# One trunk layer on one core: input tiles as 128 contiguous rows, reordered by the transposes; a bias table without its second copy in HBM; identity transposes at the start

## The chip, the cores and the metric

The kernel runs on one NeuronCore of a Trainium2 chip. A core has TensorE (PE), VectorE (DVE), ScalarE (ACT), GpSimd (POOL), a synchronisation engine (SP) that issues most DMAs, and 16 DMA engines. The time is that of the device, in microseconds (us), from launch to end. The kernel before was timed three times: 862.17, 866.29 and 864.95 us, median 864.95.

## The reference

One layer of a transformer on 128 prompt tokens and 512 sample tokens of width 1024, all in float32:

```
for each group (prompt: c_ctx; sample: c):
    sh1, sc1, gt1, sh2, sc2, gt2 = split(silu(cond) @ w_mod + b_mod, 6)       # w_mod 1024 x 6144
    h = rmsnorm(x, g_mix_pre) * (1 + sc1) + sh1
    qa, ka, va, qb, kb, vb = split(h @ w_in)                                 # w_in 1024 x 2304
    oa = 8 heads: prompt full attention; sample 2-D neighbourhood attention + cached keys
    ob = 8 heads: prompt full attention with a sink; sample window attention + rope + cached keys
    x = x + gt1 * rmsnorm(concat(rmsnorm(oa), rmsnorm(ob)) @ w_out)
    u = conv3(rmsnorm(x, g_ffn_pre) * (1 + sc2) + sh2) @ w_up ...            # w_up 1024 x 5632
    x = x + gt2 * rmsnorm((silu(gate) * val) @ w_down)                       # w_down 2816 x 1024
```

The sample tokens form a grid of 8 rows by 64 columns (token = row * 64 + column). Neighbourhood attention adds a bias to each score that depends on the row and column distance of query and key: `rpb_a[head, drow, dcol]`, 8 heads of 15 by 31 numbers; keys whose column is out of reach get a large negative number.

## The kernel before

The layer runs in stages, one after the other on the same core: loads, normalisation and transposition of x; the modulation and the V projection ("V phase"); q, k and attention of the neighbourhood heads, then of the window heads; the output projection; the FFN's first and second half. Products are made of three float32r products each, with every operand split into a high and a low part (`split`: ACT writes the high part, DVE or POOL the low).

**Token order.** Inside the kernel the sample tokens are in the order (j, r, c): 8 column blocks j of 8 columns, in each 8 rows r of 8 columns c. So 128 tokens in that order are two column blocks with all eight rows. `xnT[kb]` holds the normalised x transposed: 128 features on the partitions, 640 tokens along the row.

**The start (L174 to L326).** `load_xt(t)` brings tile t of x, 128 tokens by 1024 features, to `xs`. For the sample it makes two DMAs of 64 rows: `xsj[2 * t + jj]` picks the 8 x 8 tokens of one column block, and its outermost dimension has 8 entries. `x_norm(t)` squares and sums a tile on ACT, makes 1/rms on POOL and scales the tile on DVE. `x_trans(t)` transposes eight blocks of 128 x 128 on PE into two PSUM tiles `pxs`, which ACT and DVE copy to `xnT`. Small parameter rows (`load_rows`) come by DMAs of their own.

**The V phase (L458 to L500).** For each of eight blocks k of 128 features, PE makes two modulation products from `wm[k]` (two tiles of 512 KB; `ada_a`, `psada`), turns them to columns (`ada_c`, `pscol`), DVE makes G and S from them, ACT and DVE make h of block k (`hidden`), and 15 products go into the five V tiles `pv_` (`psv`). The V weights `vw[0..3]` are split by `vw_split`. The modulation of block k + 2 is made in the course of block k. `stream` brings the q/k weights (`wst`).

**The bias table.** `load_scr` (called at k = 4) scales `rpb_a` by 8 into `rpx`, rows of 48 numbers, in two versions v (0: columns out of reach are negative, 1: all 31 columns), and writes each version 16 times to `scr` in HBM. `load_ftab` copies `scr` to `ftab` in HBM by 1920 runs of 32 numbers for each v, with a start that moves by one number for each of the 16 copies. `load_traw(h)` reads four times 64 runs of 256 numbers from `ftab` for head h, with a start that depends on the query's column, to `traw`. `tab_ops(h)` puts `traw` in the order of the scores (`tab`), by copies on ACT and DVE for heads 0 and 1, on POOL for the others.

**What sets the order.** From the start to the end of the first q/k projection, the instructions of each engine run in the order in which the code is written (`manual_schedule`). SP issues its DMAs in that order too; a DMA waits in SP's queue until its buffer is free and until an older DMA that uses the same one of eight completion slots has landed. Behind it a scheduler orders the attention; the FFN is written out by hand again. Weight tiles have two buffers `ws0` and `ws1`, taken in turn, so `wst` of index 1 waits for the split of `vw[3]`.

## Time and profile before

| | |
|---|---|
| median of three runs | 864.95 us |
| the profiled execution's own time | 862.87 us |
| its span (first to last instruction) | 861.1 us |
| PE busy | 805.4 us (94%) |
| DVE, ACT, POOL busy | 563.5, 435.3, 305.5 us |
| moved by DMA | 107.77 MB, 125 GB/s over the span |
| mean granted TensorE clock | 0.983 |

One execution was profiled. Times in the views count from the span's start. A row of the timeline shows start, duration, engine, line and operation, then what is written and read, and in brackets how long the engine had been idle before and what ended that; a group of several equal instructions has one row, with their count. "SPq" and "ACTq" are the times in which SP or ACT issue a DMA, not the transfer. In the rows by stretch, the DMA share is the mean busy share of the 16 DMA engines. Matmul rows overlap, since PE is pipelined.

### The profile page before, as it was taken

How to read it: one execution, taken by the hardware profiler on the slowest of the kernel's cores; microseconds unless marked ns; L12 is line 12 of the kernel's file. 1: busy time of each engine (PE TensorE's matmuls, PEld its weight loads, DVE VectorE, ACT ScalarE, POOL GpSimd, SP SyncE). 2: the span in 40 equal slices, each digit the busy share in tenths (PEclk: the TensorE clock that was granted, in tenths of full speed). 3: DMA queues.
4: the chain of work that ended last, by engine and by line, in shares of the span. 5: the costliest groups of instructions: out<-in, count | busy, mean ns of one | idle time of the engine just before them, and what ended most of it. 6: DMA issues, size and time to landing. Idle time of an engine off the chain costs nothing.

```text
span 861.1 us, 13868 instructions
## 1 busy us (share of the span) xinstructions
PE 805.4 (94%) x5280; PEld 706.3 (82%) x5280; DVE 563.5 (65%) x1023; ACT 435.3 (51%) x876; POOL 305.5 (35%) x353
## 2 busy tenths in 40 slices
PE   2897999999999999999998999999999999999996
PEld 2666878888778777868898999999999987888885
DVE  1543466655788885476588898898998874422115
ACT  3443467746568786466535455455455544322112
POOL 2443144424121211155965565665665300000002
PEclk9999899999999998999999999999999999999999
DMA  6996644363522022656323332432432326434313
GB/s 152 264 234 117 169 144 126 109 175 97 134 74 74 26 74 61 213 173 188 105 65 93 116 114 83 126 113 80 128 113 83 119 101 228 170 112 159 120 49 122
DMA packets 144277, 107.77 MB, mean 125 GB/s; under 512 B 16440, under 2 KB 125268, under 8 KB 144212
## 3 DMA queue, kind: packets, MB, share of 16 engines
q1 hardware_dynamic: 143204, 106.25, 41.9%
q8 instruction: 41, 0.67, 0.3%
q10 hardware_dynamic: 1008, 0.66, 0.3%
q14 instruction: 24, 0.20, 0.1%
HBM read 93.02 MB, written 14.36 MB: 125 GB/s over the span
## 4 chain that ended last, share of the span: by engine, by line
PE 43%; DVE 30%; DMA 10%; ACT 8%; issue 5%; POOL 4%; SPq 1%; DVEq 0%; ACTq 0%; POOLq 0%
PE psd L127 16%; PE psg L127 9%; DVE cv L120 7%; DVE ou L111 5%; DVE cv L111 4%; DVE owl L111 3%; PE psya L127 3%; POOL fg L111 3%; PE psS L127 2%; PE zx L127 2%; ACT cv L108 2%; PE psyb L127 2%; DVE yy L111 2%; DMA wms<-in_w_mod_dram 2%; DMA scr<-rpx 2%
## 5 line engine op out<-in xcount | busy, mean ns | idle before, releaser
L127 PE MATMUL psd<-dwh,a 128*128 128x512 f32 x440 | 138.3, 395 | 0.0
L111 POOL TENSOR_TENSOR wsum<-wraw 128x512 f32<-128x512 f32 x36 | 78.7, 2204 | 93.7 <-DVE oc L111 86.1
L127 PE MATMUL zx<-h2H,ou 128*128 128x322 f32 x392 | 96.0, 314 | 7.2 <-DVE cv L120 4.0
L127 PEld LDWEIGHTS psd<-dwh,a 128*128 128x128 f32 x440 | 82.9, 188 | 19.8
L127 PE MATMUL psd<-dwl,a 128*128 128x512 f32 x220 | 87.2, 396 | 0.0
L127 PE MATMUL psg<-hH,wh 128*128 128x320 f32 x224 | 76.6, 342 | 8.4 <-ACT T L108 3.6
L111 DVE TENSOR_TENSOR dwl<-wd,dwh 128x1024 fp32r<-128x1024 f32 x22 | 26.9, 1224 | 86.6 <-ACT dwh L108 86.6
L127 PEld LDWEIGHTS zx<-h2H,ou 128*128 128x128 f32 x392 | 68.4, 190 | 9.6 <-DVE yy L111 5.4
L127 PE MATMUL psg<-hH,wl 128*128 128x320 f32 x224 | 71.0, 317 | 0.0
L127 PE MATMUL psg<-hL,wh 128*128 128x320 f32 x224 | 71.0, 317 | 0.0
L108 ACT ACTIVATE dwh<-wd 128x1024 fp32r<-128x1024 f32 x22 | 23.3, 1059 | 91.2 <-PE psd L127 85.5
L117 POOL TENSOR_SCALAR rdv<-ssdc 128x1 f32<-128x1 f32 x5 | 1.6, 328 | 177.3 <-ACT jk L108 177.3
L127 PE MATMUL zx<-h2L,ou 128*128 128x322 f32 x196 | 61.1, 312 | 0.0
L127 PEld LDWEIGHTS psg<-hH,wh 128*128 128x128 f32 x224 | 43.5, 194 | 17.5 <-issue 7.2
L108 ACT ACTIVATE cv<-yy,T 128x642 f32<-128x642 f32 x20 | 17.7, 886 | 67.2 <-DVE yy L111 67.2
L127 PEld LDWEIGHTS psd<-dwl,a 128*128 128x128 f32 x220 | 41.3, 188 | 10.3 <-DVE dwl L111 0.5
L120 DVE SCALAR_TENSOR_TENSOR cv<-yy,T,cv 128x641 f32<-128x641 f32 x40 | 35.4, 884 | 17.9 <-ACT cv L108 17.2
L111 POOL TENSOR_TENSOR wl<-wst,wh 128x1024 fp32r<-128x1024 f32 (+1 forms) x12 | 27.7, 2311 | 50.5 <-ACT wh L108 34.0
L127 PEld LDWEIGHTS psg<-hL,wh 128*128 128x128 f32 x224 | 43.6, 195 | 0.5
L127 PEld LDWEIGHTS psg<-hH,wl 128*128 128x128 f32 x224 | 43.4, 194 | 0.0
L111 DVE TENSOR_TENSOR ou<-wraw,ou 128x1024 fp32r<-128x1024 f32 x19 | 41.4, 2177 | 1.5 <-ACT ou L108 1.5
L108 ACT ACTIVATE P<-P,nm 128x320 f32<-128x320 f32 (+3 forms) x64 | 40.3, 630 | 3.9 <-DVE nm L639 3.8
(352 smaller groups left out, 2217.6 us busy)
## 6 DMA issues: line engine op xcount, KB each, us to landing
wraw<-in_w_up_dram SPq DMA_DIRECT2D x40, 512.0 KB
wms<-in_w_mod_dram SPq DMA_DIRECT2D x32, 512.0 KB
wd<-in_w_down_dram SPq DMA_DIRECT2D x22, 512.0 KB
wm<-in_w_mod_dram SPq DMA_DIRECT2D x16, 512.0 KB
aD<-cv SPq DMA_DIRECT2D x22, 321.0 KB
ar<-aD SPq DMA_DIRECT2D x11, 642.0 KB
wst<-in_w_in_dram SPq DMA_DIRECT2D x10, 512.0 KB
yD<-Y SPq DMA_DIRECT2D x5, 512.0 KB
```

What stands on the lines that cost most here:

```text
L108: return nc.scalar.activation(out=out, in_=in_, func=func, **kw)
L111: return (eng or nc.vector).tensor_tensor(out=out, in0=a, in1=b, op=op)
L117: return e.tensor_scalar(out=out, in0=a, scalar1=s1, scalar2=s2, op0=op0, op1=op1)
L120: return nc.vector.scalar_tensor_tensor(out=out, in0=a, scalar=s, in1=b, op0=op0, op1=op1)
L127: return nc.tensor.matmul(out, l, r, start=start, stop=stop, skip_group_check=True, **kw)
```

## The change

- x tiles: one DMA of 128 contiguous rows (two grid rows of 64 tokens) for each of the four sample tiles. The order (j, r, c) is made afterwards: a transpose of such a tile writes PSUM in runs of 8 columns (j, r, c with two rows r), and the copies to `xnT` put 16 tokens into each of the eight column blocks.
- The first loads stand in another order in SP's queue, and the first two parameter rows are transposed one tile earlier.
- 24 transposes of the identity stand first in PE's queue.
- The bias rows are stored backwards in 32 numbers a row (`rpx`), in one copy (`scr`, 2 x 8 x 512 numbers); `ftab` is gone, `load_traw` reads its runs from `scr`, and the table copies read them with a step of -1. `load_scr` is called at k = 1; `load_traw(0)` and `(1)` at k = 4.

```diff
 def load_xt(t):
-    if t == 4:
-        nc.sync.dma_start(out=xt[4], in_=xp)
-    else:
-        for jj in range(2):
-            nc.sync.dma_start(out=xt[t][jj * 64:jj * 64 + 64, :], in_=xsj[2 * t + jj])
-
-PW = 48
-rpx_ = PT([8, 2, 15, PW], "rpx")
-rpx = [rpx_[:, v] for v in range(2)]
-for v in range(2):
-    nc.gpsimd.memset(rpx[v], NEG)
+    nc.sync.dma_start(out=xt[t], in_=(xp if t == 4 else xs[t * 128:t * 128 + 128, :]))
+
+rpx = PT([8, 2, 512], "rpx")
+nc.gpsimd.memset(rpx, NEG)
...
-scr = dr_.tile([2, 16, 120, PW], F32, name="scr")
-ftab = dr_.tile([2, 16, 120 * 32], F32, name="ftab")
+scr = dr_.tile([2, 8, 512], F32, name="scr")
...
 def load_scr():
-    ts(rpx[0][:, :, 15:31], rev(rp, 7, 16), 8.0, None, ALU.mult)
-    ts(rpx[1][:, :, 8:39], rev(rp, 0, 31), 8.0, None, ALU.mult)
-    for v in range(2):
-        nc.sync.dma_start(
-            out=scr[v].rearrange("q (h a) w -> h q (a w)", h=8),
-            in_=rpx[v].rearrange("p a w -> p (a w)").unsqueeze(1).to_broadcast([8, 16, 720]),
-        )
-
-def load_ftab():
-    for v in range(2):
-        sv = scr[v, 0]
-        nc.sync.dma_start(
-            out=ftab[v].rearrange("q (a k) -> q a k", k=32),
-            in_=bass.AP(tensor=sv.tensor, offset=sv.offset + 15, ap=[[120 * PW - 1, 16], [PW, 120], [1, 32]]),
-        )
+    rv = [rpx[:, v, 0:480].rearrange("p (a w) -> p a w", w=32) for v in range(2)]
+    ts(rv[0][:, :, 16:32], rev(rp, 22, 16), 8.0, None, ALU.mult)
+    ts(rv[1][:, :, 0:31], rev(rp, 30, 31), 8.0, None, ALU.mult)
+    nc.sync.dma_start(out=scr.rearrange("v h w -> h v w"), in_=rpx)
...
-                in_=bass.AP(tensor=fv.tensor, offset=fv.offset + jj * 8 * 3840 + h * 480,
-                            ap=[[32, 8], [3840, 8], [1, 256]]))
+                in_=bass.AP(tensor=sv.tensor, offset=sv.offset + jj * 8, ap=[[32, 8], [1, 8], [1, 256]]))
...
-            nc.tensor.transpose(ps[:, i * 128:i * 128 + 128], xt[t][:, k * 128:k * 128 + 128], ident)
-        dst = xnT[kb][:, :, t * 128:t * 128 + 128]
-        src = ps.rearrange("p (k t) -> p k t", k=4)
+            o_ = ps[:, i * 128:i * 128 + 128]
+            if t < 4:
+                o_ = o_.rearrange("p (j r c) -> p r j c", j=8, r=2)
+            nc.tensor.transpose(o_, xt[t][:, k * 128:k * 128 + 128], ident)
+        if t == 4:
+            dst, src = xnT[kb][:, :, 512:640], ps.rearrange("p (k t) -> p k t", k=4)
+        else:
+            dst = xnT[kb][:, :, 0:512].rearrange("p k (j w) -> p k j w", j=8)[:, :, :, 16 * t:16 * t + 16]
+            src = ps.rearrange("p (k j w) -> p k j w", k=4, j=8)
...
+ps = PS("o", "warm")
+for i in range(24):
+    nc.tensor.transpose(ps[:, i % 4 * 128:i % 4 * 128 + 128], ident, ident)
 x_norm(0)
...
+    if k == 1:
+        load_scr()
...
     if k == 4:
-        load_scr()
-        load_ftab()
         stream.load()
         load_cc(0)
-    if k == 5:
         load_traw(0)
         load_traw(1)
...
-            src = bass.AP(tensor=b_.tensor, offset=b_.offset + 7 * 32 + j0 * 8,
-                          ap=[list(b_.ap[0]), [8, nj], [-32, 8], [1, 8]])
+            src = bass.AP(tensor=b_.tensor, offset=b_.offset + 7 * 32 + (23 if v else 31) - j0 * 8,
+                          ap=[list(b_.ap[0]), [-8, nj], [-32, 8], [-1, 8]])
```

How the queues stand before and after is shown at three places. First, SP's queue at the start of the kernel before (each row is a DMA: line, what is written from what, its shape; `xs_128` to `xs_130` are pairs of x tiles, `rows_127` the parameter rows, `wm_...` the modulation weights):

```order
L205 DMA xs_128<-in_x_sample_dram 64x1x1024 x4
L205 DMA xs_129<-in_x_sample_dram 64x1x1024 x2
L198 DMA rows_127<-in_c_ctx_dram 8x128
L198 DMA rows_127<-in_c_dram 8x128
L205 DMA xs_129<-in_x_sample_dram 64x1x1024 x2
L234 DMA wm_146<-in_w_mod_dram 128x8x128 x2
L202 DMA xs_130<-in_x_prompt_dram 128x1024
L198 DMA rows_127<-in_b_mod_dram 48x128
L198 DMA rows_127<-in_g_mix_pre_dram 8x128
L198 DMA sel<-in_sel_c_dram 128x2
L238 DMA vw<-in_w_in_dram 128x2x512
L234 DMA wm_155<-in_w_mod_dram 128x8x128 x2
```

and after the change:

```order
L200 DMA xs_128<-in_x_sample_dram 128x1024
L197 DMA rows_127<-in_c_ctx_dram 8x128
L197 DMA rows_127<-in_c_dram 8x128
L200 DMA xs_128<-in_x_sample_dram 128x1024
L200 DMA xs_129<-in_x_sample_dram 128x1024 x2
L200 DMA xs_130<-in_x_prompt_dram 128x1024
L197 DMA rows_127<-in_b_mod_dram 48x128
L197 DMA rows_127<-in_g_mix_pre_dram 8x128
L197 DMA sel<-in_sel_c_dram 128x2
L226 DMA wm_144<-in_w_mod_dram 128x8x128 x2
L230 DMA vw<-in_w_in_dram 128x2x512
L226 DMA wm_149<-in_w_mod_dram 128x8x128 x2
```

All five x tiles now stand ahead of the first modulation tile, and the first `vw` still between the first two. Behind these rows the second `vw` and the loads of `rp` and `sink` have moved ahead of the third and fourth modulation tiles.

Second, SP's queue around the bias table, before:

```order
L238 DMA vw<-in_w_in_dram 128x2x512
L350 DMA wst<-in_w_in_dram 128x8x128
L246 DMA scr<-rpx 8x16x720 x2
L254 DMA ftab<-scr 1920x1x32 x2
L350 DMA wst<-in_w_in_dram 128x8x128
L454 DMA cc<-in_cache_a_k_dram 128x128
L455 DMA cc<-in_cache_a_v_dram 128x128
L266 DMA traw_710<-ftab 64x1x256 x4
L266 DMA traw_715<-ftab 64x1x256 x4
```

and after:

```order
L238 DMA scr<-rpx 8x2x512
L230 DMA vw<-in_w_in_dram 128x2x512
L338 DMA wst<-in_w_in_dram 128x8x128 x2
L442 DMA cc<-in_cache_a_k_dram 128x128
L443 DMA cc<-in_cache_a_v_dram 128x128
L247 DMA traw_675<-scr 64x1x256 x4
L247 DMA traw_680<-scr 64x1x256 x4
L247 DMA traw_984<-scr 64x1x256 x4
L821 DMA wms<-in_w_mod_dram 128x8x128
```

The second `wst` now directly follows the first, with no bias table between them, and `traw` of the third head (`traw_984`) stands ahead of the next weights.

Third, PE's queue at the start, before:

```order
L306 MATMUL pxs<-ident,xs_128 128x128 x8
L321 MATMUL psr_220<-ident,rows_127 128x16
L306 MATMUL pxs<-ident,xs_128 128x128 x8
L306 MATMUL pxs<-ident,xs_129 128x128 x8
L383 MATMUL psada<-wm_146,cpad 32x128 x16
L306 MATMUL pxs<-ident,xs_129 128x128 x8
L329 MATMUL psr_297<-ident,rows_127 128x72
L415 MATMUL pscol<-sel,m_sb 128x2 x2
L306 MATMUL pxs<-ident,xs_130 128x128 x8
L383 MATMUL psada<-wm_155,cpad 32x128 x16
```

and after:

```order
L303 MATMUL warm<-ident 128x128 x24
L309 MATMUL psr_219<-ident,rows_127 128x16
L290 MATMUL pxs<-ident,xs_128 128x2x8x8 x16
L290 MATMUL pxs<-ident,xs_129 128x2x8x8 x8
L371 MATMUL psada<-wm_144,cpad 32x128 x16
L290 MATMUL pxs<-ident,xs_129 128x2x8x8 x8
L317 MATMUL psr_316<-ident,rows_127 128x72
L403 MATMUL pscol<-sel,m_sb 128x2 x2
L290 MATMUL pxs<-ident,xs_130 128x128 x8
L371 MATMUL psada<-wm_149,cpad 32x128 x16
```

The first modulation products still stand between the transposes of tiles 2 and 3; the transposes' shapes are new, and the rest of PE's queue is as before to the kernel's end. ACT, DVE and POOL keep their orders too, but for the parameter rows, the scaling of `rpx`, and some table copies of the third head that POOL now makes ahead of memsets.

More of the change, by code (lines that the diff above doesn't have):

```diff
@@ L177, in trunk_kernel @@
     xt = [xp_[t // 2][:, t % 2, :] for t in range(5)]
-    xsj = xs.rearrange("(r j c) d -> j r c d", r=8, j=8, c=8)
     rows = [
@@ L200, in load_xt @@
     def load_xt(t):
-        if t == 4:
-            nc.sync.dma_start(out=xt[4], in_=xp)
-        else:
-            for jj in range(2):
-                nc.sync.dma_start(out=xt[t][jj * 64:jj * 64 + 64, :], in_=xsj[2 * t + jj])
-    PW = 48
-    rpx_ = PT([8, 2, 15, PW], "rpx")
-    rpx = [rpx_[:, v] for v in range(2)]
-    for v in range(2):
-        nc.gpsimd.memset(rpx[v], NEG)
+        nc.sync.dma_start(out=xt[t], in_=(xp if t == 4 else xs[t * 128:t * 128 + 128, :]))
+    rpx = PT([8, 2, 512], "rpx")
+    nc.gpsimd.memset(rpx, NEG)
     def rev(ap, o, n):
-        return bass.AP(tensor=ap.tensor, offset=ap.offset + 14 * 31 + o, ap=[list(ap.ap[0]), [-31, 15], [1, n]])
-    scr = dr_.tile([2, 16, 120, PW], F32, name="scr")
-    ftab = dr_.tile([2, 16, 120 * 32], F32, name="ftab")
+        return bass.AP(tensor=ap.tensor, offset=ap.offset + 14 * 31 + o, ap=[list(ap.ap[0]), [-31, 15], [-1, n]])
+    scr = dr_.tile([2, 8, 512], F32, name="scr")
     wm = {}
@@ L264, in load_traw @@
             for jj in range(2):
-                fv = ftab[v]
+                sv = scr[v, h]
                 nc.sync.dma_start(
                     out=t[jj * 64:jj * 64 + 64, v, :],
-                    in_=bass.AP(tensor=fv.tensor, offset=fv.offset + jj * 8 * 3840 + h * 480,
-                                ap=[[32, 8], [3840, 8], [1, 256]]))
+                    in_=bass.AP(tensor=sv.tensor, offset=sv.offset + jj * 8, ap=[[32, 8], [1, 8], [1, 256]]))
     load_xt(0)
+    load_rows(2)
     load_xt(1)
     load_xt(2)
-    load_rows(2)
     load_xt(3)
-    load_wm(0)
     load_xt(4)
     load_rows(3)
+    load_wm(0)
     load_vw(0)
     load_wm(1)
+    load_late()
+    load_vw(1)
     load_wm(2)
-    load_vw(1)
     load_wm(3)
-    load_late()
     load_rows(6)
@@ L312, in x_trans @@
                 act(dst, src)
+    ps = PS("o", "warm")
+    for i in range(24):
+        nc.tensor.transpose(ps[:, i % 4 * 128:i % 4 * 128 + 128], ident, ident)
     x_norm(0)
-    for t in range(1, 5):
-        if t == 4:
-            break
+    for t in range(1, 4):
         x_norm(t)
-        if t == 2:
+        if t == 1:
             ps = PS("o", "psr1")
```

## The prediction, made before the changed kernel was run

> **What bounds the kernel now.** I read the page's first part, then the chain that ended last, then busy time by stretch, then the timelines of the queues around each idle place of PE.
>
> ```profile
> span 861.1 us, 13868 instructions
> PE 805.4 (94%) x5280; PEld 706.3 (82%) x5280; DVE 563.5 (65%) x1023; ACT 435.3 (51%) x876; POOL 305.5 (35%) x353
> ```
>
> PE is busy 94% of the span: 55.7 us are left in which it does nothing. The change touches only the first 95 us and the table copies after them, so what it can earn must lie there. The stretches (length; busy us of PE, PEld, DVE, ACT, POOL; granted clock; DMA share; GB/s) show where:
>
> ```profile
> 2.00:10.00 8.00, 0.00 (x0) 0.00 (x0) 0.59 (x1) 1.35 (x4) 1.32 (x3) 1.00 0.50 140
> 10.00:20.00 10.00, 5.18 (x22) 4.38 (x23) 2.95 (x6) 3.78 (x9) 1.49 (x4) 1.00 0.81 175
> 20.00:36.00 16.00, 12.44 (x138) 9.04 (x136) 8.36 (x18) 7.62 (x15) 6.13 (x11) 1.00 1.09 304
> 36.00:40.00 4.00, 4.00 (x27) 3.19 (x19) 1.41 (x4) 1.33 (x2) 3.27 (x5) 1.00 0.31 71
> 84.00:90.00 6.00, 5.08 (x19) 5.08 (x20) 4.12 (x14) 3.49 (x11) 0.00 (x0) 0.51 0.78 214
> ```
>
> From 2 to 10 us nothing but the x tiles is moved, and the 16 DMA engines are busy exactly half: 140 GB/s, where 20 to 36 us move 304. All engines idle for that: the start is bound by the loads. Which load sets PE's first real work is seen in three rows of the timeline (start, duration, idle before):
>
> ```profile
> 7.30 1.06 ACT L108 ACTIVATE junk<-xs 128x1024 fp32r<-128x1024 f32 x1 [5.08 <-DMA xs<-in_x_sample_dram]
> 29.60 0.64 PE L383 MATMUL psada<-wm,cpad 128*32 128x128 f32 x16 [0.44 <-DMA wm<-in_w_mod_dram]
> 30.41 0.50 PE L127 MATMUL psv<-vwh,hH 128*128 128x512 f32 x1 [0.16 <-ACT hH L108]
> ```
>
> The last thing ahead of the first `psv` product is the second modulation tile (`wm` of k = 1), which lands at 29.6. Behind it the V phase runs PE-bound, one k in 5.14 us, with one exception; then three idle places of PE follow:
>
> ```profile
> 50.62 1.06 ACT L108 ACTIVATE vwh<-vw 128x1024 fp32r<-128x1024 f32 x1 [3.74 <-DMA vw<-in_w_in_dram]
> 51.87 0.50 PE L127 MATMUL psv<-vwh,hx 128*128 128x512 f32 x1
> 54.19 0.51 PE L127 MATMUL psv<-vwl,hH 128*128 128x512 f32 x1 [1.15 <-POOL vwl L111]
> 58.87 0.50 PE L127 MATMUL psv<-vwh,hx 128*128 128x512 f32 x1
> 64.01 0.51 PE L127 MATMUL psv<-vwh,hx 128*128 128x512 f32 x1
> 78.01 0.39 PE L127 MATMUL psg<-hH,wh 128*128 128x320 f32 x1 [1.81 <-DVE V L111]
> 81.48 1.06 ACT L108 ACTIVATE wh<-wst 128x1024 fp32r<-128x1024 f32 x1 [4.41 <-DMA wst<-in_w_in_dram]
> 84.92 0.64 PE L127 MATMUL psg<-hH,wh 128*128 128x320 f32 x1 [2.88 <-DVE q L111]
> ```
>
> From 51.87 to 58.87 one k takes 7.00 us instead of 5.14 (64.01 − 58.87), because the third V weight tile (`vw` 2) lands at 50.6. The rest is told with the parts that touch it.
>
> **A: x tiles as 128 rows.** Eight DMAs of 64 rows become four of 128; the prompt's already has that form. What must land before `psv` starts:
>
> ```profile
> xs<-in_x_sample_dram SPq DMA_DIRECT2D x8, 256.0 KB
> wm<-in_w_mod_dram SPq DMA_DIRECT2D x16, 512.0 KB
> vw<-in_w_in_dram SPq DMA_DIRECT2D x4, 512.0 KB
> 0.72 4.04 SPq L205 DMA_DIRECT2D xs<-in_x_sample_dram  x6
> ```
>
> Five x tiles (2560 KB), `wm` of k = 0 and 1 (2048 KB) and `vw` 0 (512 KB) are the same 5120 KB in both orders. Up to 20 us the kernel moved 8 × 140 + 10 × 175 = 2870 thousand bytes; at 304 GB/s these take 9.4 us instead of 18, so the stream is 8.6 us ahead and the second `wm` lands at 21.0. SP is no limit: its six issues took 4.04 us. With one `psada` group behind it (0.64) and 0.2 of waiting, `psv` could start at 21.8. Ahead of that PE must have passed the first `wm` (2560 + 1024 KB are 3.67 MB: 12.1 us at 304, from 2.0, and some 1.5 from last byte to waiter as in the first tile, where 524 kB at 140 end at 5.7 and ACT starts at 7.3: 15.6), a `psada` group, the transposes of tile 3, the small products, the transposes of tile 4 and two more `psada`. How long these are depends on PE's pace:
>
> ```profile
> 10.22 1.97 PE L306 MATMUL pxs<-ident,xs 128*128 128x128 f32 x8 [10.22 <-DVE xs L116]
> 27.52 1.07 PE L306 MATMUL pxs<-ident,xs 128*128 128x128 f32 x8 [0.90 <-ACT vwh L108]
> 23.08 1.08 PE L383 MATMUL psada<-wm,cpad 128*32 128x128 f32 x16 [0.57 <-DMA wm<-in_w_mod_dram]
> 25.85 0.33 PE L329 MATMUL psr<-ident,rows 72*128 72x72 f32 x1
> 26.00 0.62 PE L415 MATMUL pscol<-sel,m_sb 128*128 128x2 f32 x4
> 12.04 0.58 ACT L108 ACTIVATE xnT<-pxs 128x512 f32<-128x512 f32 x1
> ```
>
> The same eight transposes take 1.97 and then 1.07, a `psada` group 1.08 and then 0.64; the small products are 1.0 together. At the quick pace PE is done with tile 4 by 19.4 and the load decides (21.8); at the slow one 15.6 + 1.1 + 2.0 + 1.0 + 2.0 + 2 × 1.1 = 23.9. The 24 identity transposes cost nothing themselves: at 0.246 each (1.97/8) they are 5.9 us of an empty queue, and the first x tile, landed at 5.2 (2.0 + 1.7 + 1.5) instead of 7.3, reaches PE only after ACT, POOL and DVE (7.30 to 10.22), at 8.1. Whether they make the pace quick I can't tell, so I take the middle, 22.9: **A = 7.5** (bounds 6.4; 10 if 340 GB/s, the best stretch, held). ACT has 1.06 + 0.58 us of work a tile, about a tile's load at 304 (1.7), so it keeps up. The transposes' outputs in runs of 8 and the copies in runs of 16 have the same element counts: 0, at most the tile-3 transposes doubled (2.0).
>
> The moves in SP's order put 512 KB (`vw` 1) ahead of the third `wm`: 1.7 us later in the stream. By the bytes it lands at about 25.9; it is wanted 4.7 us after `psv` starts, at 27: nothing.
>
> **B: the third V weight.** At 36 to 40 us the DMA engines ran 71 GB/s: SP was issuing eight small loads in a row, each of which waits for an older DMA's slot. Now two of them go earlier, and two large tiles are still in flight when the last are issued. Of the 4 × (304 − 71)/304 = 3.1 us lost there I need only one: `vw` 2 at 50.6 − 8.6 − 1 = 41.0, its split done 3.6 later (54.2 − 50.6) at 44.6; PE wants it at 54.2 − 1.15 − 7.5 = 45.5. **B = 7.00 − 5.14 = 1.8** (bounds 0.8, 1.8).
>
> **C: no ftab.** The bias table loses one round through HBM, and SP's queue a wait for it and a long issue:
>
> ```profile
> 68.23 7.65 SPq L254 DMA_DIRECT2D ftab<-scr  x2
> 72.03 4.34 ACTq L1167 DMA_DIRECT2D out_dram<-vo  x1
> 78.61 5.80 SPq L266 DMA_DIRECT2D traw<-ftab  x8
> 97.06 0.34 ACTq L593 DMA_DIRECT2D out_dram<-ko  x1
> 60.42 2.39 POOL L111 TENSOR_TENSOR vwl<-vw,vwh 128x1024 fp32r<-128x1024 f32 x1 [0.56 <-ACT vwh L108]
> 75.99 0.90 SPq L350 DMA_DIRECT2D wst<-in_w_in_dram  x1
> 72.50 0.31 PE L127 MATMUL psg<-hH,wh 128*128 128x320 f32 x1
> 75.89 0.31 PE L127 MATMUL psg<-hH,wl 128*128 128x320 f32 x1
> 84.92 10.01 PE psg L127 x48
> ```
>
> ACT issues the store of `vo` at 72.03 and is held 4.34 us, where such a store took 0.34 at 97; it gets free 0.5 us after SP's `ftab` issue ends (75.88). The split of V that PE waits for at 78.01 stands behind it. Without it that split ends 4.0 earlier, at 74, before the 24 products of 72.50 to 75.89 are through: **C = 1.8** (0 if the store is slow by itself).
>
> **D: the second q/k weight.** Its load (`wst`) stood behind `ftab` in SP's queue and left at 75.99; ACT waits 4.41 us for it, with the q split behind it, and PE 2.88 for that. Now it waits only for the split of `vw` 3 to free its buffer, and that end (62.8) comes A + B = 9.3 earlier: the load leaves at 53.5 and, with its 5.4 us (75.99 to 81.4), is there at 59; ACT wants it once V is split, at 73 − 9.3. The eight `traw` loads follow it with 5.8 us of issue, to 61, and their copies stand behind the q split that PE now waits for at 84.92, some 14 us earlier in future. **D = 2.9** (bounds 0, 2.9).
>
> **E: the clock behind that stall.** The granted clock from 84 to 90 is 0.51, and 48 products take 10.0 us; the 24 from 72.50 took 3.5, so 48 take 7.1. The stall of 1.81 did not lower the clock, that of 2.88 did. With D gone: **E = 2.9** (0 if any 2 to 3 us of idle stay).
>
> **Costs.** The two scalings of `rpx` (0.67 together) move to an earlier k, behind the `hL` of that k, where DVE waits for PE anyway: 0. The table copies read backwards, with the same elements; two of the chains run through them:
>
> ```profile
> 131.32 2.31 DMA traw<-ftab
> 135.52 0.56 DVE P L639
> L518 POOL COPY tab<-traw x30: 288/337/536, 90.6 to 165.7; 64x192 f32<-64x192 f32 x12, 64x128 f32<-64x128 f32 x12, 128x256 f32<-128x256 f32 x6
> ```
>
> At 131 and again at 161 DVE waits for the last copies. Doubled, four copies at each place cost 2.8 us; faster they can hardly be; I take 0.3. The `traw` loads read 64 overlapping runs of one 2 KB row, at any 4-byte offset: 64 KB at 140 GB/s are 0.5 of the 2.31 us, the rest is the way there and back; I take 0.2. The Trainium skill, DMA: Bandwidth & Descriptors, "How a descriptor splits into AXI transactions", says that a descriptor off a 256-byte boundary fetches from the boundary below it; by it 1 KB takes up to five transactions where it took four, an estimate of 0.1 us more in each of the two places. No row here shows the split.
>
> Sum: 7.5 + 1.8 + 1.8 + 2.9 + 2.9 − 0.5 = 16.4. Behind 95 us the order on every engine is the old one and nothing waits for a fixed time, so the shift stays. The profiled execution took 862.87, 2.1 under the median; 862.9 − 16.4 = 846.5, and on the median's scale 864.95 − 16.4 = **848.5**.
>
> **Rivals.**
> 1. The places at 76 to 95 us stay, because the store is slow for its own size (256 KB against 64) or another wait takes the weight's: C, D and E (7.6) go missing: 856.1. For it: the row of the store names no releaser. Against: its end fits `ftab`'s.
> 2. The engines, not the loads, bound the start: slow pace and tile 3 doubled, `psv` at 25.9, A = 4.5: 851.5. The Trainium skill, TensorE: Matmul & The Clock Gate, "What's actually happening", has the clock fall after an idle window of about 3.4 us; here 2.88 us sufficed. By it the identity transposes buy nothing if a pause follows: `psv` at 23.9 and 1 us more than the forecast.
> 3. The half rate of the x loads is not from their form: A is 0, and B too, since PE then wants `vw` 2 no earlier: 864.95 − 7.6 + 0.5 = 857.9. For it: 10 to 20 us, where the prompt's 128 rows also move, reach 175. Against: a share of 0.50 with nothing else moving.
> 4. Slower: the overlapping runs of `traw` are served one at a time, at one engine's eighth of 140 GB/s: 3.7 us for each DMA, 15 for a head. 131 and 161 are two heads apart, 15 us each, so the loads can't run ahead; each of the two places waits 4 × (3.7 − 0.6) = 12 us more: 848.5 + 24 = 872.5. It decides once a DMA takes over 2.7 us (16.4/2 = 8.2 a head, 2.1 on top of 0.6). For it: all 64 runs now hit one row instead of eight regions. Against: `ftab`'s runs overlapped eight deep too.
>
> **Chances.** Forecast 0.68, rivals 0.12, 0.10, 0.06, 0.04. The range reaches from A at 10 with no costs (845.5) and some of the spread of the three runs (−3) to rivals 1 and 3: 842 to 857.5. One can tell 0.5% (4.3 us) from no change here: under 860.6 lie the forecast and rivals 1 to 3, but for a small rest: faster 0.93, same 0.03, slower 0.04.
>
> **What will show it.** DMA share near 1 and about 300 GB/s from 2 us on; first `psv` at 22 to 24; no 7 us k; `vo`'s issue under 1 us; no PE wait over 1 us at the second and third `psg` group and a clock of 1.00 there; `traw` landing within 3 us. Wrong would be a first `psv` after 27, or tables that DVE waits for longer than before.

## The result, and the profile after

The changed kernel takes 850.48 us in the median of four runs (848.29 to 855.52), the kernel before 864.85 in the median of four: a ratio of 0.9855, with a 95% interval of 0.9813 to 0.9896. It is faster by 14.4 us, where 16.4 were forecast.

The profiled execution of the changed kernel is the longest of its four: 855.52 us, against 862.87 for the profiled one of before. So the two traces are only 7.5 us of span apart, and the account has to be made by stage, not from the two ends. The page of the changed kernel:

```profile
span 853.6 us, 13902 instructions
PE 806.5 (94%) x5304; PEld 708.5 (83%) x5304; DVE 564.7 (66%) x1023; ACT 436.0 (51%) x876; POOL 303.2 (36%) x352
```

PE's work is the same (24 identity transposes more). Four marks cut the execution into stages: the first V product (`psv`), the first score product of the neighbourhood heads (`psS<-k,q`), the first one of the window heads (`psS<-kvU,qb`) and the first product of the FFN's second half (`psd`).

| stage | before | after | difference |
|---|---|---|---|
| start to first V product | 30.4 | 21.8 | -8.6 |
| to the first score product | 64.5 | 56.6 | -7.9 |
| neighbourhood heads | 134.0 | 142.1 | +8.1 |
| window heads, output, FFN first half | 471.1 | 471.9 | +0.8 |
| FFN second half to the end | 161.1 | 161.2 | +0.1 |

The marks of the third and fourth stage are read from the groups of one tile (minimum, median and maximum in ns, first and last start in us). Of before:

```profile
L127 PE MATMUL psS<-kvU,qb x120: 269/389/503, 228.9 to 327.5; 64*128 64x384 f32 x48, 64*128 64x512 f32 x48, 64*128 64x128 f32 x24
```

and of the changed kernel:

```profile
L127 PE MATMUL psS<-kvU,qb x120: 268/389/502, 220.5 to 318.7; 64*128 64x384 f32 x48, 64*128 64x512 f32 x48, 64*128 64x128 f32 x24
```

So 16.5 us were won by the first score product, close to the 16.9 of the forecast, and in this pair of traces 8.1 of them were given back in a stage that the forecast held to be all but untouched. The win, by the same stretches as before (length; busy us of PE, PEld, DVE, ACT, POOL; granted clock; DMA share; GB/s):

```profile
2.00:10.00 8.00, 4.90 (x32) 4.40 (x30) 1.09 (x2) 2.51 (x6) 1.69 (x5) 1.00 0.93 320
10.00:20.00 10.00, 7.12 (x67) 5.92 (x68) 5.46 (x10) 6.71 (x15) 2.38 (x7) 0.66 1.13 311
20.00:36.00 16.00, 14.27 (x142) 10.67 (x140) 9.08 (x21) 6.37 (x12) 8.54 (x15) 0.89 1.02 269
66.00:80.00 14.00, 14.00 (x110) 13.29 (x108) 8.44 (x22) 6.78 (x20) 1.81 (x9) 1.00 0.36 103
```

The DMA engines are full from the start (0.93 at 320 GB/s where it was 0.50 at 140), and from 66 to 80 us PE has no idle place. The first x tile reaches ACT at 4.33 instead of 7.30, and none of PE's waits from 16 us to the first V product is for a load any more; the last is for ACT:

```profile
4.33 1.06 ACT L108 ACTIVATE junk<-xs 128x1024 fp32r<-128x1024 f32 x1 [2.11 <-DMA xs<-in_x_sample_dram]
14.18 1.97 PE L290 MATMUL pxs<-ident,xs 128*128 128x128 f32 x8 [2.41 <-DVE xs L116]
21.80 0.50 PE L127 MATMUL psv<-vwh,hH 128*128 128x512 f32 x1 [0.35 <-ACT hH L108]
63.58 0.43 ACTq L1154 DMA_DIRECT2D out_dram<-vo  x1
```

The last row is the store of V that held ACT for 4.34 us: its issue takes 0.43. The chain that ended last (start, duration, what) runs from the V phase to the scores without a gap, and has two waits for modulation weights behind them, where before had one:

```profile
64.19 7.06 PE psg L127 x48
71.37 7.08 PE psg L127 x48
78.44 0.65 PE psS L127 x5
79.72 6.00 DMA wms<-in_w_mod_dram
87.87 5.48 DMA wms<-in_w_mod_dram
```

A row of the chain counts the whole way of the load: PE itself was idle for it only 0.85 and 0.83 us (1.08 for the one of before).

Inside the 16.5 there is a loss that the forecast's sum does not have. The first k of the V phase, from its first product to the next k's first, takes 7.67 us, where it took 5.67 before. In the changed kernel:

```profile
23.92 0.50 PE L127 MATMUL psv<-vwh,hL 128*128 128x512 f32 x1 [1.38 <-DVE hL L111]
26.31 0.63 PE L127 MATMUL psv<-vwl,hH 128*128 128x512 f32 x1
29.47 0.50 PE L127 MATMUL psv<-vwh,hx 128*128 128x512 f32 x1
```

and in the kernel before:

```profile
36.08 0.50 PE L127 MATMUL psv<-vwh,hx 128*128 128x512 f32 x1
```

Behind a wait of 1.38 us (0.96 before) the products take 0.63 us where they take 0.40 at other times, and the granted clock is 0.72 from 24 to 26 us and 0.50 from 26 to 28. It is the 0.89 of the stretch from 20 to 36 us, which was 1.00 before. The run with one row read aligned (e1, below) has the same wait, 1.39 us, at a clock of 1.00, and its first k takes 6.08.

Now what was given back. Two of the waits of PE and DVE from 76 to 230 us in the changed kernel (total, times, longest):

```profile
PE psS L127 <- DVE nm L626: 3.0, 2, 1.5
DVE P L626 <- POOL tab L505: 4.1, 2, 2.0
```

and DVE's waits for the tables in the kernel before:

```profile
DVE P L639 <- POOL tab L518: 0.7, 2, 0.5
```

There PE never waited for `nm`. PE's idle time for the modulation weights grew as well, from 1.1 to 2.1 us. `nm` comes out of the same two-part instruction as P (scores plus table, and the row's maximum); the next score product needs the PSUM that it reads. Such a place, first in the changed kernel, then in the kernel before:

```profile
122.00 0.56 DVE L626 CUSTOM_DVE_ANT_0 P<-psS,tab 128x384 f32<-128x384 f32 x1 [2.05 <-POOL tab L505]
```

```profile
135.52 0.56 DVE L639 CUSTOM_DVE_ANT_0 P<-psS,tab 128x384 f32<-128x384 f32 x1 [0.23 <-POOL tab L518]
```

The granted clock was lower around these places. The stretch that holds the first place and the one that follows the second (its wait ends at 155.50), of the changed kernel:

```profile
110.40:125.40 15.00, 12.60 (x94) 10.48 (x94) 7.68 (x24) 9.55 (x25) 5.07 (x17) 0.95 0.54 137
155.40:170.40 15.00, 13.57 (x110) 12.20 (x110) 9.49 (x33) 9.46 (x28) 6.54 (x10) 0.89 0.38 114
```

and the stretches of the kernel before at the same distance from its own first score product, where the clock was 1.00 in the whole stage:

```profile
126.90:141.90 15.00, 14.51 (x125) 12.30 (x126) 10.27 (x33) 11.55 (x30) 4.93 (x17) 1.00 0.45 126
171.90:186.90 15.00, 15.00 (x131) 12.78 (x124) 7.79 (x29) 8.29 (x26) 5.42 (x6) 1.00 0.61 169
```

The copies that make the table are not slower: 287/340/534 ns (shortest, median, longest of the 30 on POOL), 288/337/536 before. It is their input, `traw`, that lands later. Between the copies of one head POOL waits up to 1.17 us for the last load, where it waited at most 0.62 before. For the last head, the last of the four loads is issued from 150.8 us on and its copy starts at 155.17, 4.4 us later; before it was 163.0 and 165.75, 2.7 us.

### The profile page after: what moved, and what is told of

It reads as the page before. It is cut to its first block, busy times and chain, and to the rows that moved or that the text cites. A ratio compares the mean times of both kernels' runs of the same rounds, so it can differ in the third digit from the quotient of the medians.

```text
span 853.6 us, 13902 instructions
## 1 busy us (share of the span) xinstructions
PE 806.5 (94%) x5304; PEld 708.5 (83%) x5304; DVE 564.7 (66%) x1023; ACT 436.0 (51%) x876; POOL 303.2 (36%) x352
## 4 chain that ended last, share of the span: by engine, by line
PE 48%; DVE 28%; ACT 7%; DMA 5%; issue 4%; POOL 4%; SPq 1%; DVEq 0%; ACTq 0%; POOLq 0%
PE psd L127 16%; PE psg L127 8%; DVE cv L120 7%; DVE ou L111 5%; PE psv L127 4%; DVE cv L111 3%; DVE owl L111 3%; PE zx L127 3%; POOL fg L111 3%; PE psya L127 3%; PE psyb L127 2%; DMA wms<-in_w_mod_dram 2%; PE psS L127 2%; ACT cv L108 2%; DVE yy L111 2%
## 5 line engine op out<-in xcount | busy, mean ns | idle before, releaser
L108 ACT ACTIVATE dwh<-wd 128x1024 fp32r<-128x1024 f32 x22 | 23.3, 1060 | 91.4 <-PE psd L127 85.7
L108 ACT ACTIVATE cv<-cv 128x642 f32<-128x642 f32 x22 | 16.4, 744 | 50.2 <-DVE cv L120 50.2
```

What stands on the lines that cost most here:

```text
L108: return nc.scalar.activation(out=out, in_=in_, func=func, **kw)
```

## The experiments

Theory H: `traw` lands late because all 64 runs of a load now come from one 2 KB row of `scr` in HBM, which is read again and again. Rival A: because the runs begin at any 4-byte offset. Rival W: the tables are not the cause, the given-back time is that of the modulation weights and of a clock that falls by itself. Beside that, the terms of the sum were tried: each half of the change alone, the identity transposes, the form of the x loads, and the place of the weight's load.

All times in us. The runs below a row of the kernel before were made on one chip with it and are compared with it. "Heads" is the length of the neighbourhood stage in the profiled run, "wait" what DVE waited for the tables.

| run | median (range) | ratio to before, 95% | first psv | psv to psS | heads | wait |
|---|---|---|---|---|---|---|
| *before, first comparison* | 864.85 (862.17 to 866.29) | | 30.4 | 64.5 | 134.0 | 0.7 |
| the change | 850.48 (848.29 to 855.52) | 0.9855, 0.9813 to 0.9896 | 21.8 | 56.6 | 142.1 | 4.1 |
| *before, second comparison* | 864.09 | | | | | |
| e0 the change again | 852.39 (848.06 to 854.17) | 0.9858, 0.9818 to 0.9899 | 20.5 | 56.6 | 140.4 | 3.3 |
| e1 one row, aligned | 854.21 (850.54 to 855.78) | 0.9875, 0.9836 to 0.9915 | 21.1 | 55.7 | 140.4 | 4.0 |
| e2 16 copies, unaligned | 855.72 (851.90 to 857.07) | 0.9890, 0.9849 to 0.9931 | 22.1 | 62.4 | 135.3 | 1.2 |
| e3 16 copies, aligned | 854.39 (849.70 to 860.47) | 0.9888, 0.9837 to 0.9939 | 20.7 | 65.2 | 136.1 | 0.3 |
| *before, third comparison* | 862.13 | | | | | |
| e4 no identity transposes | 851.59 (848.69 to 852.73) | 0.9854, 0.9818 to 0.9890 | 21.0 | 56.6 | 139.2 | 2.4 |
| e5 x half alone | 854.69 (850.14 to 857.87) | 0.9891, 0.9846 to 0.9937 | 21.1 | 61.6 | 134.5 | 0.3 |
| e6 bias half alone | 857.15 (853.76 to 862.13) | 0.9946, 0.9916 to 0.9975 | 31.2 | 56.1 | 138.5 | 3.2 |
| e8 x tiles as halves | 851.41, one run | | 23.3 | 56.3 | 136.6 | 1.8 |
| *before, fourth comparison* | 855.59, one run | | | | | |
| e9 before, weight first | 862.04, one run | | 28.1 | 64.4 | 134.0 | 0 |
| *before, fifth comparison* | 862.80 | | | | | |
| e10 16 copies, written later | 847.52 (841.60 to 853.19) | 0.9814, 0.9769 to 0.9859 | 20.5 | 56.8 | 136.8 | 1.2 |
| e11 8 copies, written later | 848.10 (844.45 to 851.34) | 0.9816, 0.9777 to 0.9855 | 21.4 | 55.8 | 138.2 | 1.6 |
| e12 the change again | 850.94 (844.83 to 854.76) | 0.9846, 0.9803 to 0.9889 | 22.4 | 56.7 | 135.9 | 2.6 |

**The change again.** The same kernel, run beside e1 to e3.

> The changed kernel once more, beside its variants. Its first profile was 16.5 us ahead of before at the first score product (78.4 against 94.9) and only 7.5 at the end; the median of its runs was 14.4 ahead. Theory W (the traw loads are slow and DVE waits for the tables at heads 5 and 7): again two waits of DVE for POOL's table copies near 122 and 155, about 4 us together, landings of the four traw loads of a head 1.2 to 1.4 us apart, and a time of 848 to 852. Rival N (that profile was an odd one, the waits are of that run): waits under 1 us together and a shift of 15 or more kept to the end.

It gave 11.7 us against its chip's runs of before, and e12 11.9: a little less than the 14.4 of the first comparison, with overlapping intervals. In e0 the front is much the same (first score product at 77.1), and the neighbourhood stage is long again.

**One row, aligned.** Every query column reads the same place of the row, at a multiple of 128 bytes, which is what "aligned" means here; the bias's shift by column is left out.

```diff
-in_=bass.AP(tensor=sv.tensor, offset=sv.offset + jj * 8, ap=[[32, 8], [1, 8], [1, 256]])
+in_=bass.AP(tensor=sv.tensor, offset=sv.offset, ap=[[32, 8], [0, 8], [1, 256]])
```

> The 64 runs of a traw load start at multiples of 128 bytes, as ftab's runs did, but all in one row of 2 KB as in the changed kernel: eight of them are now the same run (the shift by the query's column is left out, so the bias is not the reference's). Theory A (the 4-byte offsets make the runs dear): the four loads of a head land 0.6 to 0.7 us apart as before the change, DVE's two waits shrink to under 1 us together, 3 to 5 us faster than the changed kernel, about 846. Rival H (64 runs from one row are served slowly): landings stay 1.2 us or more apart and the time within 1 us of the changed kernel.

Without the odd offsets nothing came back: DVE waited 4.0 us for the tables, the stage took 140.4. From the groups of `tab`, the list of who waited for it (us, times):

```profile
  DVE P L626: 4.0, 2
```

**Sixteen copies, unaligned and aligned.** `scr` is written in sixteen copies of 17 KB each, and every column reads its own; in the first kernel at the same odd offsets as in the change, in the second the shift is made when the copies are written, and all reads are aligned. The diff shows the first of the two.

```diff
-scr = dr_.tile([2, 8, 512], F32, name="scr")
+scr = dr_.tile([2, 16, 8, 544], F32, name="scr")
-nc.sync.dma_start(out=scr.rearrange("v h w -> h v w"), in_=rpx)
+for v in range(2):
+    nc.sync.dma_start(out=scr[v, :, :, 0:512].rearrange("q h w -> h q w"),
+                      in_=rpx[:, v].unsqueeze(1).to_broadcast([8, 16, 512]))
...
-offset=sv.offset + jj * 8, ap=[[32, 8], [1, 8], [1, 256]]
+offset=sv.offset + jj * 8 * (8 * 544 + 1), ap=[[32, 8], [8 * 544 + 1, 8], [1, 256]]
```

> scr is written 16 times, 17 KB apart, and each of the eight columns reads its own copy, at the same 4-byte offsets as in the changed kernel; no second pass, same order on all engines. Rival H (one hot row): the loads land 0.6 to 0.7 us apart, 3 to 5 us faster than the changed kernel, about 846. Theory A (4-byte offsets): no change in the landings (1.2 us or more apart), time within 1 us of the changed kernel.

> As the one with 16 copies, but each copy is written shifted by its number, so that every run of a traw load starts at a multiple of 128 bytes: what ftab gave, without the second pass. Theory A and rival H both expect landings 0.6 to 0.7 us apart and 3 to 5 us less than the changed kernel (about 846). If it is no faster, the traw loads are not what gave the shift back.

In the heads both did what H says: the wait of P for the tables fell to 1.2 and 0.3 us, the stage to 135.3 and 136.1. Between odd and aligned offsets there is no difference in the stage that can be told from the spread of the runs. The same list, unaligned and aligned, and from the timeline of the aligned one the last copy of a head on POOL:

```profile
  DVE P L629: 1.2, 2
```

```profile
  DVE P L631: 0.3, 1
```

```profile
157.06 0.29 POOL L510 COPY tab<-traw 64x128 f32<-64x128 f32 x1 [0.20 <-DMA traw<-scr]
```

and the last copy of that head in the changed kernel:

```profile
155.17 0.29 POOL L505 COPY tab<-traw 64x128 f32<-64x128 f32 x1 [1.17 <-DMA traw<-scr]
```

But the times, expected at some 846 us by H, did not improve, for a reason that neither theory had: the way from the first V product to the first score product became 6 to 9 us longer. The write of 512 KB stands in SP's queue ahead of the last V weight. In the unaligned kernel, the timelines of SP, ACT and PE, and the stretch:

```profile
42.27 1.37 SPq L239 DMA_DIRECT2D scr<-rpx  x2
43.73 3.99 SPq L230 DMA_DIRECT2D vw<-in_w_in_dram  x1
56.56 1.06 ACT L108 ACTIVATE vwh<-vw 128x1024 fp32r<-128x1024 f32 x1 [5.32 <-DMA vw<-in_w_in_dram]
58.05 0.50 PE L127 MATMUL psv<-vwh,hH 128*128 128x512 f32 x1 [1.22 <-ACT hH L108]
60.10 0.80 PE L127 MATMUL psv<-vwl,hH 128*128 128x512 f32 x1 [1.54 <-POOL vwl L111]
```

```profile
56.00:64.00 8.00, 5.24 (x15) 3.55 (x16) 2.42 (x4) 2.42 (x4) 3.66 (x5) 0.70 0.42 120
```

The weight is split at 56.56, PE idles, and the clock falls to 0.70. In the changed kernel the split began 5.7 us earlier:

```profile
50.82 1.05 ACT L108 ACTIVATE vwh<-vw 128x1024 fp32r<-128x1024 f32 x1
```

What the copies gave back to the heads, their write took from the V phase.

**Without the identity transposes.** The 24 transposes ahead of the first x tile are left out of the changed kernel.

```diff
-ps = PS("o", "warm")
-for i in range(24):
-    nc.tensor.transpose(ps[:, i % 4 * 128:i % 4 * 128 + 128], ident, ident)
```

> The changed kernel without the 24 identity transposes. If they make PE quick at the start (the changed kernel's transposes of tiles 0, 3 and 4 took 1.1 us, those of tile 2 1.97): the transposes of tiles 0, 3 and 4 take 2.0 us, the first psv product starts 1 to 2 us later than 21.8, the time is 1 to 2 us longer. If the loads alone decide: first psv within 0.3 us, same time.

The ratio is the same (0.9854), and the first V product starts at 20.98, within the 20.5 to 22.4 of the three profiled runs with them:

```profile
13.35 1.97 PE L290 MATMUL pxs<-ident,xs 128*128 128x128 f32 x8 [1.74 <-DVE xs L116]
20.98 0.50 PE L127 MATMUL psv<-vwh,hH 128*128 128x512 f32 x1 [0.35 <-ACT hH L108]
```

With the identity transposes the first group of eight is quick (1.09) and the third slow again (1.97 at 14.18, above): between them lie pauses of 2.13 and 2.41 us, and the granted clock is 0.66 from 10 to 20 us. That the pauses undo the identity transposes is likely and not shown: in e4 the first three groups all take 1.97 at a granted clock of 1.00. They buy nothing that can be measured.

**The halves alone.** The x half (row form of the tiles, order of the loads, identity transposes, with the old bias table), and the bias half (the new table and its calls, with the old x loads). Together they are the diff of the change.

> The kernel before with the x tiles of 128 rows, the new order of the first loads and the identity transposes, but the old bias table with scr and ftab at k = 4. My sum: A and B alone, first psv at 22, no k of 7 us, then the same waits at the second and third psg group and the slow clock as before (C, D, E stay): 862.9 - 9.3 gives 855 on the median's scale, 9 to 10 us faster than before, all of it kept to the end since the traw loads are the old ones. Rival: ftab meets a later stage of the loads and the waits grow: 857 or more.

> The kernel before with the new bias table alone; x and the first loads as before. My sum: first psv at 30.4, the k of 7 us stays, C, D and E are gone: first score product 7.6 us earlier (87.3 instead of 94.9), of which the slow traw loads give back 3 to 6: 859 to 862, 3 to 6 us faster than before. If the two halves of the change add up, its gain and that of the x half sum to the whole's (14.4).

The x half earns 7.4 us (0.9891), the bias half 5.0 (0.9946); their sum, 12.4, agrees within the uncertainty with the 10.5 of e4, which on that chip stands for the change. Of the x half 9 to 10 were expected. Its profiled run, the fastest of its four, was 12.2 us ahead at the first score product and 12.7 at the end, the median 7.4: the median gain falls short of a profiled front even where the tables cost nothing (0.3). In the x half PE's two idle places at the second and third group of q/k products are still there:

```profile
67.88 0.38 PE L127 MATMUL psg<-hH,wh 128*128 128x320 f32 x1 [1.65 <-DVE V L111]
75.42 0.41 PE L127 MATMUL psg<-hH,wh 128*128 128x320 f32 x1 [2.93 <-DVE q L111]
```

```profile
75.42 7.33 PE psg L127 x48
```

The last row is from the chain that ended last: behind a stall of 2.93 us the 48 products took 7.33, not 10.01. In the bias half both places are gone (chain, second fence), and the wait for the third V weight is still there (timeline, first fence):

```profile
54.68 0.51 PE L127 MATMUL psv<-vwl,hH 128*128 128x512 f32 x1 [1.25 <-POOL vwl L111]
```

```profile
73.13 7.05 PE psg L127 x48
80.29 7.07 PE psg L127 x48
```

**x tiles as two halves.** As the change, but each x tile comes in two DMAs of 64 contiguous rows: as many DMAs as before, of the same size, only the row pattern is new.

```diff
-nc.sync.dma_start(out=xt[t], in_=(xp if t == 4 else xs[t * 128:t * 128 + 128, :]))
+if t == 4:
+    nc.sync.dma_start(out=xt[4], in_=xp)
+else:
+    for jj in range(2):
+        o = t * 128 + jj * 64
+        nc.sync.dma_start(out=xt[t][jj * 64:jj * 64 + 64, :], in_=xs[o:o + 64, :])
```

> The changed kernel with each sample tile loaded by two DMAs of 64 contiguous rows. If the half rate before came from the source's outermost dimension of 8 (64 rows as 8 groups of 8): full rate, 300 GB/s and a DMA share near 1 from 2 to 10 us, first psv within 0.5 us of the changed kernel's 21.8. If it came from writing 64 partitions at a time: 140 GB/s and a share of 0.5 as before, first psv near 29 to 30.

The first stretch, and from the timeline the first tile on ACT:

```profile
2.00:10.00 8.00, 6.04 (x32) 5.37 (x30) 0.75 (x1) 2.50 (x6) 1.56 (x5) 1.00 1.00 225
```

```profile
5.75 1.06 ACT L108 ACTIVATE junk<-xs 128x1024 fp32r<-128x1024 f32 x1 [3.54 <-DMA xs<-in_x_sample_dram]
```

The DMA engines are busy all the time (1.00 instead of 0.50): the half-idle engines were a matter of the pattern. The rate is 225 GB/s, between 140 and 320, and the first tile is at ACT at 5.75, between 7.30 and 4.33. So the pattern explains about half of the higher rate, and the size of the DMA (256 or 512 KB) seems to be the rest; this is one run. The first V product came at 23.3, 0.9 to 2.8 us later than in the runs with whole tiles.

**The weight ahead of the table, in the kernel before.** In the unchanged kernel only the second q/k weight is moved ahead of `load_scr` and `load_ftab`, to try D alone.

```diff
 if k == 4:
+    stream.load()
     load_scr()
     load_ftab()
-    stream.load()
     load_cc(0)
```

> The kernel before with one line moved: at k = 4 the second q/k weight is issued ahead of scr and ftab, so ftab is issued some 3.5 us later (from about 72 to 79 instead of 68.2 to 75.9). My account of C (ACT's issue of the vo store is held until SP's ftab issue ends): the store's issue grows from 4.3 us to about 7 and ends with ftab's near 79, and PE waits some 5 us for V at the second psg group instead of 1.8, while no wait for the weight is left (D and E as such are gone, but a stall this long may lower the clock as well). If the store is slow for its own size: its issue stays at 4.3 us, PE waits 1.8 us there and nothing at the third group, 5 to 6 us less at the first score product.

ACT's store and SP's `ftab` issue, and PE's two places:

```profile
69.07 8.34 ACTq L1167 DMA_DIRECT2D out_dram<-vo  x1
69.78 7.61 SPq L254 DMA_DIRECT2D ftab<-scr  x2
79.05 0.61 PE L127 MATMUL psg<-hH,wh 128*128 128x320 f32 x1 [5.81 <-DVE V L111]
88.81 0.41 PE L127 MATMUL psg<-hH,wh 128*128 128x320 f32 x1 [0.94 <-DVE q L111]
```

The wait for the weight went from 2.88 to 0.94, and the other from 1.81 to 5.81. The store's issue, begun a little ahead of `ftab`'s, ends at 77.41, and `ftab`'s at 77.39: ACT was held for as long as SP issued. One run of each kernel on that chip (862.04 and 855.59) says little of the time, but the stage does: moving the load gained nothing (64.4 us from the first V product to the first score product, 64.5 before). Of the kernels tried, only those without the table's second copy are rid of both waits.

**Copies written behind the weights.** To keep what the copies gave to the heads without the V phase's loss, their write is issued behind the last V weight and the first q/k weights; with sixteen copies as in e2, and with eight.

```diff
 if k == 1:
-    load_scr()
 if k == 2:
     load_vw(3)
     stream.load()
+    load_scr()
```

> The sixteen copies of the bias rows as in the run e2, one per offset, but their write is issued behind the last V weight and the first loads of the score projection's weights instead of ahead of them. If one shared row is what makes the bias loads slow, and the write's place is what cost the V phase its time, the V product's waits at 58 to 60 us (1.22 and 1.54) and the granted clock of 0.70 there are gone, the first score product starts near 77 as in the repeat of the change, not near 85, the P instruction waits at most 1.2 us for the table, not 3.3, and the median is 3 to 5 us below that of the repeat in the same comparison: 847 to 849 where the repeat gives 852. Rival: the 512 KB of the write cost their 5 us wherever they stand, since they then hold up the weights of the score projection or the bias loads themselves: PE waits at the score projection (64 to 78 us) or the first score product comes after 80, and the median is within 1 us of the repeat or above it.

> As the run before, with eight copies instead of sixteen: both halves of a load read the same copy at offsets 8 words apart, the write is 256 KB. If a row is slow in proportion to how many places it is read from at once, eight rows are as good as sixteen (P waits at most 1.2 us for the table) and the write is cheaper by half: the same median as with sixteen or up to 1 us less. If it is the traffic on the page or region of memory and not on the row, eight is worse: P waits over 2 us.

> The change once more, for the comparison on this chip: 849 to 853, first score product at 77 to 78.5, P waiting 3.3 to 4.1 us for the table.

The V phase is whole again (56.8 and 55.8 us from the first V product to the first score product, 62.4 in e2). The same stretch as above, and the list of who waited for `tab`, for sixteen copies:

```profile
56.00:64.00 8.00, 7.97 (x39) 6.44 (x38) 3.89 (x11) 4.46 (x9) 4.39 (x14) 1.00 0.55 150
```

```profile
  DVE P L628: 1.2, 1
```

The medians, 847.52 and 848.10, are the lowest of all kernels here: 15.3 and 14.7 us under before, and 3.4 and 2.8 under the repeat of the change on the same chip (850.94). But six runs of each spread over 7 to 12 us, and the means of the sixteen copies and the repeat differ by 2.8 with a standard error of 2.2: that the copies beat the change is not shown. Eight copies, with a wait of 1.6, fell between the two outcomes that were told apart (at most 1.2, over 2). The repeat missed its expectation, with a wait of 2.6 and a first score product at 79.1; its heads took only 135.9 us, so the same kernel varies there by 6 us from run to run.

**What follows.** On the waits, H holds against A: with one row read aligned DVE waits 4.0 us (e1), with many rows read at odd offsets 1.2 (e2). Over all profiled runs, the seven that read one row waited 1.8 to 4.1 us for the tables, the seven that read several rows 0 to 1.6. PE, which this reaches by way of `nm`, waited 0.8 to 3.1 us against 0 to 0.7. The loads themselves tell it most plainly: in the last three heads, from the issue of a head's four loads to its last table copy, it takes 5.2 to 6.6 us with one row and 3.2 to 5.3 with several, also in e10 and e11, whose front is that of the change. Whether it is the row of 2 KB or the stretch of memory around it was not separated.

What that costs in time is less certain. The neighbourhood stage took 139.0 us in the mean with one row against 135.6, a difference of 3.5 with a 95% interval of 1.2 to 5.7. But one thing differs beside the rows: five of the seven kernels with several rows reach the stage late, at 82.7 us or behind it, and six of the seven with one row before 80. Only e10 and e11 have several rows and an early start, and their stage took 136.8 and 138.2, inside the 135.9 to 142.1 of the six. A straight-line fit to the table's fourteen profiled runs, with the start of the stage as a second cause, gives one row 2.4 us (0.1 to 4.7) and each microsecond of earlier start 0.19. So part of what was won ahead of the heads is lost in them whatever the table; by what is not known. W is not wrong either: two runs of the same kernel, the change and e12, differ by 6 us in this stage, and only part of that lies in the waits for the tables (4.1 against 2.6 of DVE's time, 3.0 against 1.5 of PE's). In the rest the granted clock was lower (0.95, 0.94 and 0.89 against 1.00 in single stretches), and PE waited 2.1 us for modulation weights against 1.0. What lets the clock fall in one run and not in another stays open.

## Why the prediction was right, and where it was not

The forecast of 848.5 was 2.0 us from the measured median, and 850.48 lies in the range of 842 to 857.5. Part of that closeness is luck, as the sum of the front shows. By its own steps:

- **A (7.5, bounds 6.4 and 10)**: right in mechanism, a little small. The first V product came 8.6 us earlier in the profiled run, 8.0 to 9.9 in the repeats; with the old x loads it started at 30.4, 31.2 and 28.1 in three profiled runs, so the size is known to some 2 us. The share and rate of the first 10 us are as said (0.93, 320). Of the two limits weighed, PE's pace decided in the profiled run: PE has no idle place from 14.18 to 21.5, at the slow pace for a part of that, and waits for no load there. That 21.8 is also what the loads alone gave in the sum is chance. Rival 2 (25.9) did not happen, rival 3 (the half rate is not from the form) falls by e8.
- **B (1.8)**: right. The k that took 7.00 takes 5.14 in the change (45.26 to 50.40), and with the bias half alone the wait for the third V weight is still there. With the x half alone this k takes 6.15, with another wait, of 0.74 for DVE. The sign "no 7 us k" failed all the same, by the first k with its 7.67.
- **C (1.8) and D (2.9)**: right. With the x half alone both places stay (1.65, 2.93), with the bias half alone both are gone. In e9 ACT's store ends with SP's `ftab` issue, as it did before and in the x half, and rival 1 falls. The two are coupled, which the prediction did not say: in e9, relieving one place loaded the other.
- **E (2.9)**: right in size for these two traces (10.01 to 7.08), wrong in its reason as a rule. In the x half alone a stall of 2.93 us left the clock at 1.00, and 48 products took 7.33. So E is not the price of such a stall in every run.
- **Sum of the front**: 16.9 without the costs; measured at the first score product, 94.93 − 78.44 = 16.5. The terms gave more than they were put at: A 8.6, B 1.9, C to E together 8.0. What brought the sum down is the first k, 2.0 us longer at a low granted clock, which the prediction left out.
- **The costs (0.5)**: the step that failed. The reversed copies cost nothing (0.3 assumed). The `traw` loads, for which 0.2 stood, cost 3.4 us of DVE's waits in the profiled run (4.1 − 0.7) and 3.0 of PE's, and 0.8 to 3.1 of PE's in all runs with one row. The stage as a whole is longer by 3.5 us (1.2 to 5.7), or by 2.4 (0.1 to 4.7) where its start is counted too. Rival 4 had the mechanism, loads slow because all of their runs hit one row, but a price of 3.7 us for each load, worked out as if one engine read it alone; POOL waited about one microsecond for the last load of a head, so it did not decide the sign. The sentence on 256-byte boundaries (the Trainium skill, DMA: Bandwidth & Descriptors, "How a descriptor splits into AXI transactions") is not tested by these runs: the runs of `ftab` and of the aligned kernels begin at multiples of 128 bytes, so half of them were off such a boundary already. The estimate's "where it took four" is wrong for that half.
- **"The shift stays" behind 95 us**: this sentence failed with it. Of the profiled run's 16.5 us, 2 are missing in the median of the first comparison, and 4 to 5 in those of the two repeats (11.7 and 11.9). How much of that is the tables stays open, since the x half, with its old tables, also shows 7.4 in the median behind a profiled front of 12.2.
- **What would be wrong** named "tables that DVE waits for longer than before": this came true (0.7 to 4.1). "`traw` landing within 3 us" failed with it (4.4 us for the last load of the last head). The first V product at 21.80 was a little ahead of the 22 to 24. The rate of the first loads, `vo`'s issue and the second and third `psg` group came as forecast.
- **The identity transposes**: they bought nothing (0.9854 without them, 0.9855 and 0.9858 with them), as rival 2 has it where a pause follows. The Trainium skill, TensorE: Matmul & The Clock Gate, "What's actually happening", gives about 3.4 us as the idle window behind which the clock falls; the pauses here were shorter (1.44, 2.13 and 2.41 us), and the third group was slow all the same, so this trace does not agree with that length.

## What to carry to other kernels

A load's pattern can leave half of the DMA engines idle, and the DMA share of a stretch in which nothing else moves shows it; ask of each early load whether all engines work for it. Before a copy in HBM is taken away because it costs a round trip, ask whether it also spread the reads over several rows, and if the copies are kept for that, put their write behind the loads that PE waits for next. Where two waits hang on one long issue in a queue, moving one load around it only hands the wait to the other: take the issue away.

## What the runs showed of the hardware

- ACT's issue of a 256 KB store lasts as long as SP is issuing a DMA of many short runs: 4.34 us in the kernel before, 4.17 with the x half, 8.34 in e9, each time to within half a microsecond of the end of SP's issue, and 0.37 to 0.44 in the runs without it.
- Loads whose 64 runs of 1 KB lie in one 2 KB row land later than loads from several rows, whether the runs begin at odd offsets or at multiples of 128 bytes: 5.2 to 6.6 us from the issue of four such loads to the last copy, against 3.2 to 5.3.
- The granted clock did not follow the length of a stall: 0.51 behind one of 2.88 us, 1.00 behind one of 2.93, 0.70 around two of 1.22 and 1.54.
- A write of 512 KB ahead of a weight in the same queue made that weight's split start 5.7 us later (56.56 against 50.82).
- x loads in the pattern of eight groups of eight rows kept the DMA engines half busy (0.50 at 140 GB/s); 64 contiguous rows in a DMA of the same size gave 1.00 at 225 GB/s (one run), 128 rows 0.93 at 320.
